# Rows of 1/rms through a store and a load in DRAM, in a two-layer decoder trunk

## The chip, the cores and the metric

The kernel runs on one core of a Trainium2 chip. The metric is the device time of one launch in microseconds (us). The engines are named as in the profile: PE (matrix products), PEld (loading of the stationary operand, beside PE), DVE (VectorE), ACT (ScalarE), POOL (GpSimd) and SP (SyncE, which only issues transfers here). Each engine takes its instructions in one order; transfers are issued by SP, POOL and once by ACT.

## The reference

The input x has 512 tokens of 1024 values. A layer, run twice, is three residual steps, and every step begins with the same norm:

```
r(x) = x * rsqrt(mean(x*x) + 1e-6) * g
x = x + 1/2 * (silu(r(x) @ Wg) * (r(x) @ Wu)) @ Wd        ffn1, inner width 2816
x = x + concat(A, B, C)(r(x) @ Win) @ Wout                mixer, three head groups
x = x + 1/2 * (silu(r(x) @ Wg') * (r(x) @ Wu')) @ Wd'     ffn2
```

After the second layer comes one more norm. What matters here is 1/rms = rsqrt(mean(x*x) + 1e-6), one number for each of the 512 tokens, needed six times: for ffn1, mixer and ffn2 of each layer. (The last norm is computed in another way and isn't touched.)

## The kernel before, in words

The activations stand with features on the partitions and tokens along the free dimension, so x is eight tiles of 128 x 512, held in four pairs. Every product is made of three matmuls of split operands (a high and a low part each). 1/rms of a token commutes with a product over the features, so the kernel multiplies by the gains first, starts the products at once, and puts 1/rms on the results. Two forms of it are kept:

- `rc`, the columns: 128 x 4, token 128n+p at partition p and column n. `norm_columns` (L221 to L231) makes it: eight small matmuls (L226) sum the squares `acc` over the partitions into a PSUM bank, DVE divides and adds epsilon (L228), and POOL raises to the power -0.5 (L230).
- `rr`, the rows: 128 x 512, the 512 values along the free dimension, the same on all partitions. `norm_rows` (L233 to L244) makes it from `rc`: for each of the four column groups DVE multiplies the identity by a column (L240, tile `dg`), PE multiplies a matrix of ones by that diagonal (L241, into the PSUM tile `psr`), and ACT copies the bank into `rr` (L243).

The feed-forward step (`ffn`, `gate_up`) works through 22 "quads" of weight blocks, gate and up in turn. For a quad SP and POOL fetch the weights (`fetch`, L111 to L116, `rawq`, two buffers; the POOL transfer of L112 adds into what SP has brought), ACT and DVE split them (`forms`, L89 and L90, into `wd`, `wa`, `wb`), PE makes seven products (L257 to L259, Strassen style, on the banks `pa`, `pb`, `pc`), and ACT and DVE gather them (`after`, L326 to L338) into a tile `g` or `u`, of which there are two each. When a quad is complete, `done` (L341 to L356) follows. For a gate quad DVE multiplies by `rr` (L347), ACT applies silu (L348) and DVE multiplies by `rr` again (L349). For an up quad DVE multiplies by the gate (L352) and the result is split into `h`. Products of `h` with the down weights (`pdn`) are threaded between the quads at written times (`schedule`).

Where the norm is made is set by the list `norms`: after each product one entry is taken from it and called. In the first feed-forward step of the kernel (`start`) the first two quads are computed from the input in another way, and `done` of both is itself an entry of that list; in the other three the list holds `norm_columns` at the third place and `norm_rows` at the sixth. In the mixer (`mixing`) the columns follow the first projection and the rows the second (L623 to L626); the first users of `rr` there are two multiplications of cosine and sine (L632, L633), which every query and key head needs, while `rc` scales the token-major projections. Instructions are put on their engines in an order that the tile framework chooses from the program's order and from what is ready.

Of the kernel before, what the change touches and what calls it, by code (L numbers as in the profile page):

```python
# [9 lines left out]
F32 = mybir.dt.float32  # L10
F32R = mybir.dt.float32r
AF = mybir.ActivationFunctionType
ALU = mybir.AluOpType
AX = mybir.AxisListType

P = 128
D = 1024
T = 512
# [4 lines left out]
NCH = T // P  # L23
# [25 lines left out]
def trunk(ctx, tc, xt, w_gu1, w_dn1, w_in, w_out, w_gu2, w_dn2, w_last, par, con, wst, bst, gain, out):  # L49
    nc = tc.nc  # L50
# [2 lines left out]
    wpool = ctx.enter_context(tc.tile_pool(name="wpool", bufs=1))  # L53
    spool = ctx.enter_context(tc.tile_pool(name="spool", bufs=2))
    pp = ctx.enter_context(tc.tile_pool(name="pp", bufs=8, space=bass.MemoryType.PSUM))
    stage = {}

    def bank(name):
        return pp.tile([P, T], F32, tag="ps", name=name)
# [6 lines left out]
    def uniq(s):  # L66
        uid[0] += 1
        return f"{s}{uid[0]}"
# [8 lines left out]
    ones = cpool.tile([P, P], F32, name="ones")  # L77
# [5 lines left out]
    ident = cpool.tile([P, P], F32, name="ident")  # L83
# [73 lines left out]
    state = {}  # L157
# [12 lines left out]
    def scratch(i, name):  # L170

        if stage["tags"] is None:
            return big(uniq(name))
        if i == 2:
            return stage["pool"].tile([P, 4 * T], F32, tag="hp", name=uniq(name), bufs=4)
        return stage["pool"].tile([P, 2 * T], F32, tag=stage["tags"][i], name=uniq(name), bufs=2)
# [55 lines left out]

    def norm_rows():  # L233

        rc = state["rc"]
        pr = bank(uniq("psr"))
        dg = scratch(2, "dg")
        for n in range(NCH):
            d = dg[:, n * P : (n + 1) * P]
            nc.vector.tensor_scalar(d, ident, rc[:, n : n + 1], None, ALU.mult)  # L240
            nc.tensor.matmul(pr[:, n * P : (n + 1) * P], lhsT=ones, rhs=d, start=True, stop=True)  # L241
        rr = spool.tile([P, T], F32, tag="rr", name=uniq("rr"), bufs=1)
        nc.scalar.copy(rr, pr)  # L243
        state["rr"] = rr  # L244


# [37 lines left out]
    def gate_up(w_gu, first, others, tail, from_start=False):  # L284
# [73 lines left out]
        if from_start:  # L358
            norms = start(w_gu, live, done)
            skip = lambda q, n: q < 2  # L360
        else:
            begin(0)
            begin(1)
            for m in range(KP):
                for q in (0, 1):
                    for n in (1, 2):
                        ps = psum(q, ("pa", "pb")[n - 1])
                        hi, lo = live[q]["w"][n]
                        bh, bl = form(m, MOVING[n])
                        c = slice(m * P, (m + 1) * P)  # L370
                        mm3(ps, hi[:, c], lo[:, c], bh, bl, m == 0, m == KP - 1, skip_group_check=True)
            for q in (0, 1):
                for n in (1, 2):
                    after(q, n)
            wait = lambda: None
            norms = [wait, wait, norm_columns, wait, wait, norm_rows]
            skip = lambda q, n: q < 2 and n < 3
        for _, kind, q, n in steps:
            if kind:
# [12 lines left out]
    def start(w_gu, live, done):  # L392
# [37 lines left out]
            squares(m)  # L430

        def rows():
            norm_rows()
            done(0)
            done(1)

        wait = lambda: None
        return [wait] * 5 + [norm_columns] + [wait] * 2 + [rows]

    def schedule(l, w_dn, hs):  # L440

# [134 lines left out]
    def mixing(l, after):  # L576
# [22 lines left out]
        def project(block, name):  # L599

            hi, lo = load(w_in[l, block])
            p = bank(uniq(name))
            for k in range(KT):
                c = slice(k * P, (k + 1) * P)
                mm3(p, hi[:, c], lo[:, c], xh(k), xl(k), k == 0, k == KT - 1)
            return p
# [15 lines left out]
        head = lambda w, h: qk[2 * w + h // 2][:, (h % 2) * T : (h % 2 + 1) * T]  # L622
        ahead = [project(0, "pqk")]  # L623
        norm_columns()
        ahead.append(project(1, "pqk"))
        norm_rows()  # L626
        rc, rr = state["rc"], state["rr"]
        for w in range(2):
            for h in range(HEADS):
# [16 lines left out]
        for n in range(NCH):  # L646
            p = bank(uniq("psc"))
# [248 lines left out]
```

## Time and profile before

| | us |
|---|---|
| median of 3 runs (1818.01 to 1818.21) | 1818.18 |
| the profiled execution, its own time | 1819.83 |
| span of the profiled execution | 1818.1 |
| mean granted TensorE clock, share of full | 0.998 |

The profile is of one execution. Times inside it count from the start of its span. A group of instructions has its line in the kernel, engine, operation and `out<-in` by the program's names; "x48" is a count. In the timeline the first number is the start and the second how long it took; what stands in brackets is the engine's idle time before it and what ended that. The chain is the work that ended last, followed back from the end of the kernel to what released each step.

### The profile page before, as it was taken

What the parts mean: (1) busy time and instruction counts of PE and PEld (TensorE: products, weight loads), DVE (VectorE), ACT (ScalarE), POOL (GpSimd) and SP (SyncE); (2) the same over time, 40 slices, a digit from 0 to 9 for tenths busy, and PEclk for the clock granted to TensorE, in tenths of its full rate; (3) what the DMA queues carried; (4) which work ended last, traced back from release to release, by engine and by line L of the source; (5) the groups of instructions that cost most, each with busy time, mean ns of one, the idle gap of its engine ahead of it and who ended that gap; (6) DMA issues with size and microseconds to landing.
All of it is one profiled execution on the core that took longest, in us unless ns stands there. A gap on an engine that the chain in (4) does not pass through costs nothing.

```text
span 1818.1 us, 28679 instructions
## 1 busy us (share of the span) xinstructions
PE 1804.7 (99%) x11704; PEld 1652.5 (91%) x11704; DVE 1329.5 (73%) x1818; ACT 830.8 (46%) x1222; POOL 121.0 (7%) x120
## 2 busy tenths in 40 slices
PE   9999999999999999999999999999999999999998
PEld 8999999888889999999899999998888899999997
DVE  7877777675667877777888777766658688777765
ACT  7544444423345544444655444444143555444444
POOL 0100000000100000000000000000000000000000
PEclk9999999999999999999999999999999999999999
DMA  7665555522222855555447555563222157565632
GB/s 215 175 174 150 147 149 152 177 88 82 70 93 76 214 152 151 157 157 156 128 130 192 147 148 151 151 189 116 100 75 80 58 134 199 155 157 157 157 88 81
DMA packets 120339, 251.20 MB, mean 138 GB/s; under 512 B 9744, under 2 KB 11792, under 8 KB 119696
## 3 DMA queue, kind: packets, MB, share of 16 engines
q1 hardware_dynamic: 96672, 204.25, 35.0%
q0 software_dynamic: 23392, 45.09, 15.0%
q8 instruction: 91, 1.49, 0.3%
q14 instruction: 40, 0.33, 0.1%
q10 hardware_dynamic: 144, 0.04, 0.0%
HBM read 247.24 MB, written 2.10 MB: 137 GB/s over the span
## 4 chain that ended last, share of the span: by engine, by line
PE 96%; DVE 2%; ACT 1%; issue 0%; DMA 0%; POOL 0%; POOLq 0%; SPq 0%; ACTq 0%
PE pa L257 9%; PE pa L259 9%; PE pa L258 9%; PE pdn L150 8%; PE pdn L151 8%; PE pdn L152 8%; PE pc L258 4%; PE pc L259 4%; PE pc L257 4%; PE pb L257 2%; PE pb L259 2%; PE pb L258 2%; PE pqk L150 2%; PE pqk L152 2%; PE pout L151 2%; PE pout L150 2%
## 5 line engine op out<-in xcount | busy, mean ns | idle before, releaser
L150 PE MATMUL pdn<-h,wdn 128*128 128x512 f32 x632 | 247.6, 392 | 0.0
L151 PE MATMUL pdn<-h,wdn 128*128 128x512 f32 x632 | 247.6, 392 | 0.0
L152 PE MATMUL pdn<-h,wdn 128*128 128x512 f32 x632 | 246.0, 389 | 0.3 <-DVE wdn L90 0.3
L89 ACT CAST wd<-rawq 128x1024 fp32r<-128x1024 f32 (+1 forms) x172 | 135.2, 832 | 172.0 <-PE pc L259 167.4
L257 PE MATMUL pa<-xf,wa 128*128 128x256 f32 x688 | 195.5, 284 | 0.8 <-ACT g L326 0.8
L258 PE MATMUL pa<-xf,wa 128*128 128x256 f32 x688 | 194.9, 283 | 0.0
L259 PE MATMUL pa<-xf,wa 128*128 128x256 f32 x688 | 194.9, 283 | 0.0
L90 DVE TENSOR_TENSOR wd<-rawq,wd 128x1024 fp32r<-128x1024 f32 (+1 forms) x172 | 157.5, 955 | 49.1 <-ACT wd L89 48.7
L112 POOL DMA_DIRECT2D rawq<-in_w_gu x86 | 94.3, 1096 | 1260.6 <-DMA rawq<-in_w_gu 436.6
L89 ACT CAST wdn<-rawd 128x512 fp32r<-128x512 f32 (+1 forms) x152 | 97.2, 640 | 176.8 <-PE pdn L152 174.1
L89 ACT CAST w<-raw 128x1024 fp32r<-128x1024 f32 x77 | 80.9, 1051 | 196.1 <-PE pqk L152 60.6
L152 PEld LDWEIGHTS pdn<-h,wdn 128*128 128x128 f32 x632 | 118.7, 188 | 26.5 <-DVE wdn L90 0.7
L90 DVE TENSOR_TENSOR w<-raw,w 128x1024 fp32r<-128x1024 f32 x77 | 94.1, 1223 | 64.4 <-ACT w L89 63.7
L150 PEld LDWEIGHTS pdn<-h,wdn 128*128 128x128 f32 x632 | 119.2, 189 | 21.1
L151 PEld LDWEIGHTS pdn<-h,wdn 128*128 128x128 f32 x632 | 119.2, 189 | 19.5
L257 PEld LDWEIGHTS pa<-xf,wa 128*128 128x128 f32 x688 | 132.4, 192 | 1.8 <-ACT g L326 1.2
L90 DVE TENSOR_TENSOR wdn<-rawd,wdn 128x512 fp32r<-128x512 f32 (+1 forms) x152 | 107.2, 705 | 35.3 <-ACT wdn L89 35.2
L259 PEld LDWEIGHTS pa<-xf,wa 128*128 128x128 f32 x688 | 132.3, 192 | 0.0
L258 PEld LDWEIGHTS pa<-xf,wa 128*128 128x128 f32 x688 | 132.3, 192 | 0.0
L282 DVE SCALAR_TENSOR_TENSOR x<-pdn,x 128x512 f32<-128x512 f32 x152 | 104.0, 685 | 3.8 <-PE pdn L152 3.8
L90 DVE TENSOR_TENSOR wa<-rawq,wa 128x1024 fp32r<-128x1024 f32 x86 | 104.9, 1219 | 1.8 <-ACT wa L89 1.8
L90 DVE TENSOR_TENSOR wb<-rawq,wb 128x1024 fp32r<-128x1024 f32 x86 | 104.8, 1219 | 1.2 <-ACT wb L89 1.2
(289 smaller groups left out, 5080.5 us busy)
## 6 DMA issues: line engine op xcount, KB each, us to landing
rawq<-in_w_gu SPq DMA_DIRECT2D x172, 512.0 KB, 5.4
rawq<-in_w_gu POOLq DMA_DIRECT2D x86, 512.0 KB, 5.7
rawd<-in_w_dn SPq DMA_DIRECT2D x140, 256.0 KB, 4.4
raw<-in_w_in SPq DMA_DIRECT2D x52, 512.0 KB, 3.5
rawq<-in_w_gu SPq DMA_DIRECT2D x86, 256.0 KB, 5.8
raw<-in_w_out SPq DMA_DIRECT2D x16, 512.0 KB, 3.5
rawd<-in_w_dn SPq DMA_DIRECT2D x12, 384.0 KB, 3.3
raw<-in_w_last SPq DMA_DIRECT2D x6, 512.0 KB, 4.0
```

Of the source, the lines that this page charges most:

```text
L89: nc.scalar.copy(hi, src)
L90: nc.vector.tensor_tensor(lo, src, hi.bitcast(F32), ALU.subtract)
L112: nc.gpsimd.dma_start(two[:, :, 1, :], src.rearrange("p (n s c) -> p n s c", n=2, s=2)[:, :, 0, :], accum_op=ALU.add)
L150: nc.tensor.matmul(ps, lhsT=ah, rhs=bh, start=first, stop=False, **kw)
L151: nc.tensor.matmul(ps, lhsT=ah, rhs=bl, start=False, stop=False, **kw)
L152: nc.tensor.matmul(ps, lhsT=al, rhs=bh, start=False, stop=last, **kw)
L257: nc.tensor.matmul(ps, lhsT=hi[:, c], rhs=bh, start=one, stop=False, skip_group_check=True)
L258: nc.tensor.matmul(ps, lhsT=hi[:, c], rhs=bl, start=False, stop=False, skip_group_check=True)
L259: nc.tensor.matmul(ps, lhsT=lo[:, c], rhs=bh, start=False, stop=m == pairs[-1], skip_group_check=True)
L282: nc.vector.scalar_tensor_tensor(x[d], p, 0.5, x[d], ALU.mult, ALU.add)
```

## The change

`norm_rows` no longer uses DVE, PE and ACT. POOL issues a store of the 128 x 4 columns to a tile in DRAM, laid out so that the 512 values follow each other, and SP issues a load of these 2 KB onto each of the 128 partitions. The rows are now made right after the columns in all six places: in the three later feed-forward steps this moves `norm_rows` three entries earlier; in the first one the columns go one entry later and `done` of the first two quads two entries later; in the mixer the rows are made before the second projection, and a third projection is put ahead of the first use of `rr`.

```diff
+    dpool = ctx.enter_context(tc.tile_pool(name="dpool", bufs=2, space=bass.MemoryType.DRAM))
...
     def norm_rows():
-        rc = state["rc"]
-        pr = bank(uniq("psr"))
-        dg = scratch(2, "dg")
-        for n in range(NCH):
-            d = dg[:, n * P : (n + 1) * P]
-            nc.vector.tensor_scalar(d, ident, rc[:, n : n + 1], None, ALU.mult)
-            nc.tensor.matmul(pr[:, n * P : (n + 1) * P], lhsT=ones, rhs=d, start=True, stop=True)
+        row = dpool.tile([NCH, P], F32, tag="row", name=uniq("row"))
+        nc.gpsimd.dma_start(row.rearrange("n p -> p n"), state["rc"])
         rr = spool.tile([P, T], F32, tag="rr", name=uniq("rr"), bufs=1)
-        nc.scalar.copy(rr, pr)
+        nc.sync.dma_start(rr, row.rearrange("n p -> (n p)").unsqueeze(0).broadcast_to([P, T]))
         state["rr"] = rr
...
-            norms = [wait, wait, norm_columns, wait, wait, norm_rows]
+            norms = [wait, wait, lambda: (norm_columns(), norm_rows())]
...
         def rows():
-            norm_rows()
             done(0)
             done(1)
...
-        return [wait] * 5 + [norm_columns] + [wait] * 2 + [rows]
+        return [wait] * 6 + [lambda: (norm_columns(), norm_rows())] + [wait] * 3 + [rows]
...
         ahead = [project(0, "pqk")]
         norm_columns()
+        norm_rows()
         ahead.append(project(1, "pqk"))
-        norm_rows()
+        ahead.append(project(2, "pqk"))
         rc, rr = state["rc"], state["rr"]
```

## Rows read from the trace of the kernel before

**Rows 1.** The page, part 1: busy time and share of each engine.
```profile
PE 1804.7 (99%) x11704; PEld 1652.5 (91%) x11704; DVE 1329.5 (73%) x1818; ACT 830.8 (46%) x1222; POOL 121.0 (7%) x120
```
**Rows 2.** The page, part 4: shares of the chain that ended last.
```profile
PE 96%; DVE 2%; ACT 1%; issue 0%; DMA 0%; POOL 0%; POOLq 0%; SPq 0%; ACTq 0%
```
**Rows 3.** Waits of PE: us in total, times, longest.
```profile
PE pss L226 <- DVE acc L219: 0.9, 1, 0.9
PE pa L257 <- ACT g L326: 0.8, 1, 0.8
```
**Rows 4.** Tiles psr and dg: count, ns least/median/most, first and last start.
```profile
L241 PE MATMUL psr<-dg,ones x48: 270/275/275, 52.1 to 1479.2; 128*128 128x128 f32 x48
L240 DVE TENSOR_SCALAR dg<-ident,rc x24: 277/282/289, 50.1 to 1473.4; 128x128 f32<-128x128 f32 x24
```
**Rows 5.** The chain in order of time, pieces of psr: start, us.
```profile
373.61 0.89 PE psr L241 x8
...
581.90 0.22 PE psr L241 x2
...
583.40 0.67 PE psr L241 x6
```
**Rows 6.** Timeline of a later feed-forward norm (ffn2 of the first layer).
```profile
575.63 1.03 POOL L230 TENSOR_TENSOR rc<-ms,mhalf 128x4 f32<-128x4 f32 x1 [3.52 <-DVE ms L228]
...
581.92 0.37 SPq L111 DMA_DIRECT2D rawq<-in_w_gu  x1
...
585.95 1.23 DVE L347 TENSOR_TENSOR g<-g,rr 128x1024 f32<-128x1024 f32 x1 [0.87 <-ACT g L338]
...
587.42 1.22 DVE L90 TENSOR_TENSOR wa<-rawq,wa 128x1024 fp32r<-128x1024 f32 x1
...
591.11 0.28 PE L257 MATMUL pa<-xf,wa 128*128 128x256 f32 x1
```
**Rows 7.** Timeline of the first mixer's norm.
```profile
368.27 1.04 POOL L230 TENSOR_TENSOR rc<-ms,mhalf 128x4 f32<-128x4 f32 x1 [5.14 <-DVE ms L228]
...
375.91 0.69 DVE L632 TENSOR_TENSOR side<-ct,rr 128x512 f32<-128x512 f32 x1
```
**Rows 8.** The page, parts 3 and 6: a queue; issues, KB each, us to landing.
```profile
q0 software_dynamic: 23392, 45.09, 15.0%
...
rawq<-in_w_gu POOLq DMA_DIRECT2D x86, 512.0 KB, 5.7
...
raw<-in_w_in SPq DMA_DIRECT2D x52, 512.0 KB, 3.5
```
**Rows 9.** DMA issues of the whole span, further down the list.
```profile
out<-o SPq DMA_DIRECT2D x8, 256.0 KB, 2.2
```
**Rows 10.** DMA issues in the stretch 46 to 58 us alone.
```profile
rawd<-in_w_dn SPq DMA_DIRECT2D x2, 256.0 KB, 6.7
```
**Rows 11.** Timeline of the first norm of the kernel (POOL, DVE and ACT).
```profile
48.09 1.96 POOL L230 TENSOR_TENSOR rc<-ms,mhalf 128x4 f32<-128x4 f32 x1 [8.26 <-DVE ms L228]
51.48 1.14 POOL L112 DMA_DIRECT2D rawq<-in_w_gu  x1 [1.43 <-DMA rawq<-in_w_gu]
...
53.81 2.36 DVE L347 TENSOR_TENSOR g<-g,rr 128x1024 f32<-128x1024 f32 x2 [0.34 <-ACT rr L243]
...
56.31 1.06 ACT L348 ACTIVATE g<-g 128x1024 f32<-128x1024 f32 x1
...
57.40 1.23 DVE L349 TENSOR_TENSOR g<-g,rr 128x1024 f32<-128x1024 f32 x1 [0.84 <-ACT g L348]
...
59.68 1.22 DVE L352 TENSOR_TENSOR u<-u,g 128x1024 f32<-128x1024 f32 x1
...
61.88 0.36 ACT L326 COPY g<-pa 128x256 f32<-128x256 f32 x1
```
**Rows 12.** Windows: stretch, us; PE, PEld, DVE, ACT, POOL busy; clock, DMA share, GB/s.
```profile
48.00:51.00 3.00, 3.00 (x17) 3.00 (x16) 2.02 (x5) 0.00 (x0) 1.96 (x1) 0.50 0.78 236
51.00:51.40 0.40, 0.40 (x4) 0.40 (x4) 0.40 (x4) 0.00 (x0) 0.00 (x0) 0.52 1.06 353
```

## The prediction

> **What bounds the kernel now.** I read the shares by engine first, then the chain, then what PE waits for. PE shows as busy for 99% of the span [rows 1], and the chain that ended last runs through PE for 96% of it [rows 2]: this is a PE-bound kernel, and a PE instruction taken out is worth its own step, as long as nothing that PE needs becomes late. Since a busy PE can hide stalls inside its pipeline, the list of its waits is the better witness: at the two places that concern us, both behind the first norm, there are only 0.9 us before the sums of squares and 0.8 us before a product that needs a bank read out by ACT [rows 3]. In the five later norms PE stops for nothing that touches the norm. So there are two regimes: five norms in a stretch where PE alone counts, and the first norm, which stands on the chain with POOL, DVE and ACT.
>
> **What is removed.** The 48 matmuls of `psr` are eight per norm at 275 ns, but matmuls overlap, so their duration isn't their price [rows 4]. The chain shows the step: 0.89 us for eight in a mixer, 0.22 + 0.67 = 0.89 us in a feed-forward norm [rows 5]. Five later norms give 5 x 0.89 = **4.45 us**. The 24 DVE multiplications of 0.28 us [rows 4] and the six ACT copies lie beside PE and give nothing by themselves; DVE stood idle while it waited for the columns anyway.
>
> **What is added: the row's way through DRAM.** No store of four-byte pieces is in this trace, so I bound it. A POOL transfer of 512 KB lands 5.7 us after its issue [rows 8]. That queue's 23392 packets took 15.0% of 16 engines' 1818 us, which is 4363 us or 0.187 us per packet [rows 8]; 86 transfers make 272 packets each, 17 per engine, 3.2 us; so 2.5 us are left that don't depend on the size. The new store has 512 pieces, 32 per engine and one at the end. If a four-byte packet took as long as a 2 KB one, the store would land after 2.5 + 33 x 0.187 = 8.7 us. From below, the kernel's output store lands in 2.2 us [rows 9]. I take 2.5 us and 0.05 us per packet, **4.2 us**, nearer to the lower end because four bytes are little to move. The load of 2 KB onto 128 partitions is 256 KB: a 512 KB weight load lands in 3.5 us in quiet, a 256 KB one in 6.7 us in the crowded stretch behind the first norm, and 2.2 us is the fastest transfer of all [rows 8 to 10]. I take **3.5 us**. The row is then there 7.7 us after the columns, with 4.4 and 15.4 us as the ends.
>
> **The three later feed-forward norms.** Take the one at 575 us [rows 6]. The columns end at 575.63 + 1.03 = 576.66 us, and the first user of the row starts at 585.95 us, which becomes 585.06 us when PE is 0.89 us quicker: 8.4 us after the columns. The row at 7.7 us is in time, by 0.7 us. If it is later, DVE waits, and what is late next is the split of `wa` that stands behind on DVE: it ends at 588.64 us and PE uses it at 591.11 us, so another 2.5 us are free. PE is touched only when the row takes over 10.9 us. SP now waits for the store before it issues the load, and behind that wait stands the next weight fetch at 581.92 us; the store has landed by 576.66 + 4.2 = 580.9 us, so the fetch isn't held (at the upper end it is, by 3.4 us). Moving the rows three entries earlier costs nothing: the queue slots it passes on PE and DVE are its own. Cost taken: nothing.
>
> **The two mixers.** The first user of the row starts 6.6 us after the columns [rows 7], so a row after 7.7 us is 1.1 us late for DVE. The third projection, put ahead of it, gives PE work that needs no row, and the projections have banks to stand in. I cost it at nothing; with the cover gone it is at most that lateness.
>
> **The first norm.** Here the row matters at once. POOL ends the columns at 50.05 us; today DVE uses the row at 53.81 us, and from there runs the way on which PE waits: first multiplication (half of 2.36 = 1.18 us), silu 1.06, second multiplication 1.23, gate times up 1.22, then the ACT copy of 0.36 us that can only write its tile when the gate has been used; it ends at 61.88 + 0.36 = 62.24 us [rows 11], and PE's 0.8 us of waiting ends there [rows 3]. The bare links sum to 5.05 us; today they are spread over 8.4 us because other work of DVE and ACT stands between. After the change that other work can be done while the row is on its way, so I take the bare links. The load shares the stretch with weight transfers: I put it at 4.4 us, a quarter of the way from 3.5 to 6.7, since by the time the store has landed, at 54.3 us, most of these are through. The row is there at 50.05 + 4.2 + 4.4 = 58.65 us, and PE is released at 63.7 us instead of 62.24: **1.5 us later**. POOL's weight transfer at 51.48 us [rows 11] goes behind the store and is about as late as that takes to issue, some 1.1 us by its own row; the splits it feeds come after the hole anyway. Now PE's own gains in this stretch: the eight matmuls, and the 0.9 us before the sums, which the later place of the columns may remove. They only make PE reach the hole sooner, so I count them as nothing; if the row came early they would count.
>
> The clock belongs here too. After PE's stop at the sums, the granted clock fell to 0.50 for 48 to 51 us, and 0.52 until 51.4 [rows 12], the lower of its two levels, 1.2 GHz. Half speed for 3.4 us costs 1.7 us. The hole in front of the released product will be some microseconds long, longer than the stop that preceded this drop, so I expect one such stretch behind it: **1.7 us**, with 0 and 3.4 as the ends.
>
> **The sum.** 4.45 saved, 1.5 + 1.7 lost: 1.25 us less. The profiled execution took 1819.83 us for a span of 1818.1; the sum on it gives 1818.6. That execution stands 1.65 us above the median of the runs, 1818.18, so the forecast for the median is **1816.9 us**, 0.07% less: no change, within the 0.2% (3.6 us) that a measurement of this kernel can tell.
>
> **The rivals.**
>
> *The start is covered (faster).* If the row needs about 6.3 us, it is there at 56.3 us, PE is released at 61.35 us, 0.9 us earlier than today, and there is no hole to lower the clock: 4.45 + 0.9 = 5.3 us less, 1812.9. For it speaks that the fastest transfers land in 2.2 us, against it the crowd in the first norm's stretch. The Trainium skill, page "DMA: Bandwidth & Descriptors", section "Anatomy of one DMA", fits 2.0 us plus bytes over 436e3 per transfer: by it the store takes 2.0 and the load 2.6 us (estimates), the row is there at 54.7 us, and the time would be about 1811. The POOL row, with 2.5 us besides its packets, agrees with that constant roughly; the 6.7 us of the weight load do not.
>
> *The store is slow (slower).* One mechanism: 512 pieces of four bytes land late, and four feed-forward norms wait for the row. Let it need X us after the columns. The first norm loses 50.05 + X + 5.05 - 62.24 + 1.7 = X - 5.4, the three others X - 10.9 each above that, and 4.45 come back. The total passes 3.6 us slower at X = 11.5. At X = 14 it is 8.6 + 9.3 - 4.45 = 13.4 us slower, 1831.6. For it speaks the upper end of the store, against it that the end takes four bytes for as dear as 2 KB. The same page of the Trainium skill, section "Rules for kernel authors", speaks against this change: a strided last dimension lowers to one descriptor per element, and one should rearrange it. No run here shows what such an element costs.
>
> *The freed time isn't returned.* If DVE or the weight loads set the pace right behind the five norms, nothing comes back there and the start's 3.2 us remain: 1821.4. Against it: PE's list of waits has no entry there [rows 3].
>
> **How the numbers follow.** The forecast has 0.38 (rows between 7 and 11 us, a range of its own of 1814.5 to 1818.5), the covered start 0.37, the slow store 0.20, the time not returned 0.05. Faster by over 0.2% is the covered start, 0.37; within 0.2% the forecast and the time not returned, 0.43; slower 0.20. The range that leaves out 2 in 10 goes down to 1812.0, past the covered start's own value, and up to 1823.5, where the row needs about 12 us: most of the slow store lies above.
>
> **What would show it.** PE without `psr`, and five norms in which PE's waits stay empty; the user of the row in the norm near 575 us waiting for ACT, as now, and not for a transfer; the store landing near 4.2 us and the load near 3.5; behind the first norm a hole in PE of several microseconds that a transfer ends through DVE and ACT, and a stretch at half clock after it. I am wrong if that hole is not there, if the store takes 7 us or more, or if PE waits in the later norms.

## The result and the profile after

The changed kernel takes 1871.08 us (median of four runs, 1869.29 to 1872.78) beside 1818.2 us for the kernel before on the same chip (1818.01 to 1818.29): a ratio of 1.0284, with 1.0271 to 1.0296 as the 95% interval. It is 52.9 us slower; forecast were 1816.9 us, with 1823.5 as the upper end of the range. The profiled span is 1870.8 us instead of 1818.1. Beside the experiments below the kernel before was run again; its runs lie near 1818 or near 1820 us, with medians of 1818.4 to 1819.9, and the ratios there are to these.

The first two lines are from the page of the kernel after: busy time and share of each engine, and the shares of the chain that ended last.

```profile
PE 1816.3 (97%) x11656; PEld 1659.5 (89%) x11656; DVE 1321.8 (71%) x1794; ACT 827.7 (44%) x1216; POOL 126.7 (7%) x126
...
PE 87%; DMA 6%; DVE 4%; ACT 1%; issue 1%; POOL 1%; SPq 0%; POOLq 0%; DVEq 0%; ACTq 0%
```

PE has 48 instructions fewer than in [rows 1], as meant, yet is busy 11.6 us longer (part of its work runs at half clock, as shown below), and transfers, which held 0% of the chain in [rows 2], now hold 6% of it. Next, the waits of PE in the kernel after (us in total, times, longest), which answer to [rows 3]:

```profile
PE pqk L153 <- DVE w L91: 17.2, 2, 8.8
PE pa L253 <- ACT g L322: 11.5, 3, 4.4
PE pa L253 <- DVE u L330: 9.9, 1, 9.9
...
PE pa L253 <- ACT u L322: 2.5, 3, 1.6
```

The two long waits for `w` are the two mixers, the 9.9 us for `u` are the first norm, and those for ACT's copies of `pa` follow the three later feed-forward norms. All six norms stop PE, where before there were only the two stops of 0.9 and 0.8 us at the first. The issues of the two new transfers (KB each, median us from issue to landing) show why the row is late:

```profile
rr<-row SPq DMA_DIRECT2D x6, 256.0 KB, 4.8
row<-rc POOLq DMA_DIRECT2D x6, 2.0 KB, 8.6
```

The store of 2 KB takes almost twice as long as the load of 256 KB. Three timelines show what became of it. The first norm of the kernel after, to be held against [rows 11]:

```profile
48.49 1.96 POOL L231 TENSOR_TENSOR rc<-ms,mhalf 128x4 f32<-128x4 f32 x1 [8.21 <-DVE ms L229]
50.76 0.83 POOL L237 DMA_DIRECT2D row<-rc  x1 [0.30 <-POOL rc L231]
...
61.41 0.34 SPq L239 DMA_DIRECT2D rr<-row  x1
...
65.01 2.36 DVE L343 TENSOR_TENSOR g<-g,rr 128x1024 f32<-128x1024 f32 x2 [10.49 <-DMA rr<-row]
...
67.29 0.41 DVE L330 TENSOR_TENSOR u<-u,pa 128x256 f32<-128x256 f32 x1
...
67.76 0.58 PE L253 MATMUL pa<-xf,wb 128*128 128x256 f32 x1 [9.85 <-DVE u L330]
```

The norm of the second feed-forward block of layer 0, to be held against [rows 6]:

```profile
597.62 1.03 POOL L231 TENSOR_TENSOR rc<-ms,mhalf 128x4 f32<-128x4 f32 x1 [3.62 <-DVE ms L229]
599.01 0.83 POOL L237 DMA_DIRECT2D row<-rc  x1 [0.36 <-POOL rc L231]
...
607.70 0.34 SPq L239 DMA_DIRECT2D rr<-row  x1
608.14 0.38 SPq L112 DMA_DIRECT2D rawq<-in_w_gu  x1
...
614.17 1.23 DVE L343 TENSOR_TENSOR g<-g,rr 128x1024 f32<-128x1024 f32 x1 [7.09 <-DMA rr<-row]
...
616.80 0.58 PE L253 MATMUL pa<-xf,wa 128*128 128x256 f32 x1 [4.32 <-ACT g L322]
```

And the first mixer, to be held against [rows 7]:

```profile
379.24 1.04 POOL L231 TENSOR_TENSOR rc<-ms,mhalf 128x4 f32<-128x4 f32 x1 [5.99 <-DVE ms L229]
380.65 0.83 POOL L237 DMA_DIRECT2D row<-rc  x1 [0.37 <-POOL rc L231]
...
390.36 0.33 SPq L239 DMA_DIRECT2D rr<-row  x1
...
394.60 0.69 DVE L628 TENSOR_TENSOR side<-ct,rr 128x512 f32<-128x512 f32 x1 [14.09 <-DMA rr<-row]
...
403.38 1.23 DVE L91 TENSOR_TENSOR w<-raw,w 128x1024 fp32r<-128x1024 f32 x1
...
404.66 0.79 PE L153 MATMUL pqk<-xf,w 128*128 128x512 f32 x1 [8.76 <-DVE w L91]
```

The row is used 14.6, 15.5 and 14.3 us after the columns end (65.01 - 50.45, 614.17 - 598.65, 394.60 - 380.28), where 7.7 us were forecast. In the mixer, look at what stands between 394.60 and 403.38 us: 13 DVE instructions, all of them users of the row or of what is made from it, and only then the split of the next projection's weights, for which PE has been waiting.

The clock adds its part. Windows of the kernel after around that stop (columns as in [rows 12], so the granted clock is the third number from the end):

```profile
394.00:399.00 5.00, 1.90 (x9) 1.24 (x7) 4.34 (x7) 1.05 (x1) 0.00 (x0) 1.00 0.02 7
399.00:404.00 5.00, 0.00 (x0) 0.00 (x0) 4.88 (x8) 0.00 (x0) 0.00 (x0) 0.66 0.00 0
404.00:409.00 5.00, 4.34 (x10) 3.47 (x11) 4.94 (x8) 0.00 (x0) 0.00 (x0) 0.50 0.34 105
409.00:414.00 5.00, 5.00 (x19) 3.98 (x18) 2.32 (x4) 1.06 (x1) 0.00 (x0) 0.81 0.64 212
```

While PE stands still the granted clock falls, and it is at 0.50, the level of 1.2 GHz, when PE starts again at 404.66 us; it is back only within the last window. By an estimate from these windows 4.34 x 0.50 + 5 x 0.19 = 3.1 us go this way, on top of the stop of 8.8 us; less the 0.9 us of the matmuls that is the mixer's loss, 11.0.

To see where the 52.7 us of span lie, I took the start of the `rc` instruction on POOL at each norm, and the distances between them. This measure is used for every run below.

| stretch | before | after | difference |
|---|---|---|---|
| start to first norm | 48.09 | 48.49 | +0.40 |
| first norm to first mixer | 320.18 | 330.75 | +10.57 |
| first mixer to the norm of ffn2, layer 0 | 207.36 | 218.38 | +11.02 |
| to the norm of ffn1, layer 1 | 345.15 | 352.10 | +6.95 |
| to the second mixer | 342.99 | 348.44 | +5.45 |
| second mixer to the norm of ffn2, layer 1 | 207.29 | 217.84 | +10.55 |
| to the end | 347.04 | 354.80 | +7.76 |

So the first norm has cost 10.6 us, the two mixers 21.6, and the three later feed-forward norms 20.2, each net of PE's saved steps.

### The profile page after: what moved, and what is told of

It reads as the page before. It is cut to its first block, busy times and chain, and to the rows that moved or that the text cites. A ratio compares the mean times of both kernels' runs of the same rounds, so it can differ in the third digit from the quotient of the medians.

```text
span 1870.8 us, 28569 instructions
## 1 busy us (share of the span) xinstructions
PE 1816.3 (97%) x11656; PEld 1659.5 (89%) x11656; DVE 1321.8 (71%) x1794; ACT 827.7 (44%) x1216; POOL 126.7 (7%) x126
## 3 DMA queue, kind: packets, MB, share of 16 engines
q1 hardware_dynamic: 97536, 205.82, 34.5%
q0 software_dynamic: 23584, 45.11, 15.1%
## 4 chain that ended last, share of the span: by engine, by line
PE 87%; DMA 6%; DVE 4%; ACT 1%; issue 1%; POOL 1%; SPq 0%; POOLq 0%; DVEq 0%; ACTq 0%
PE pdn L151 8%; PE pdn L152 8%; PE pdn L153 8%; PE pa L253 8%; PE pa L255 8%; PE pa L254 8%; PE pc L255 4%; PE pc L253 4%; PE pc L254 4%; DMA row<-rc 3%; DMA rawq<-in_w_gu 2%; PE pb L255 2%; PE pb L254 2%; PE pb L253 2%; PE pout L151 2%; PE pout L153 2%
## 5 line engine op out<-in xcount | busy, mean ns | idle before, releaser
L253 PE MATMUL pa<-xf,wa 128*128 128x256 f32 x688 | 198.1, 288 | 14.1 <-ACT g L322 11.5
L254 PE MATMUL pa<-xf,wa 128*128 128x256 f32 x688 | 196.8, 286 | 0.0
L255 PE MATMUL pa<-xf,wa 128*128 128x256 f32 x688 | 196.8, 286 | 0.0
L253 PEld LDWEIGHTS pa<-xf,wa 128*128 128x128 f32 x688 | 134.1, 195 | 16.4 <-ACT g L322 12.4
L255 PEld LDWEIGHTS pa<-xf,wa 128*128 128x128 f32 x688 | 134.2, 195 | 0.0
L254 PEld LDWEIGHTS pa<-xf,wa 128*128 128x128 f32 x688 | 134.2, 195 | 0.0
L343 DVE TENSOR_TENSOR g<-g,rr 128x1024 f32<-128x1024 f32 x44 | 53.8, 1225 | 90.9 <-ACT g L334 60.6
L253 PE MATMUL pa<-xf,wb 128*128 128x256 f32 x344 | 98.2, 286 | 9.9 <-DVE u L330 9.9
L91 DVE TENSOR_TENSOR wa<-rawq,wa 128x1024 fp32r<-128x1024 f32 x86 | 104.9, 1219 | 3.1 <-ACT wa L90 3.1
```

Of the source, the lines that this page charges most:

```text
L91: nc.vector.tensor_tensor(lo, src, hi.bitcast(F32), ALU.subtract)
L253: nc.tensor.matmul(ps, lhsT=hi[:, c], rhs=bh, start=one, stop=False, skip_group_check=True)
L254: nc.tensor.matmul(ps, lhsT=hi[:, c], rhs=bl, start=False, stop=False, skip_group_check=True)
L255: nc.tensor.matmul(ps, lhsT=lo[:, c], rhs=bh, start=False, stop=m == pairs[-1], skip_group_check=True)
L343: nc.vector.tensor_tensor(c3, c3, rr, ALU.mult)
```

## The experiments

Each group asks one thing. The kernels have the numbers that the expectations use (there is no fifth). Distances are those of the table, in its order from the first norm on, unless a run's own are given.

### Is the wait for the row the whole loss?

In the third kernel nothing is stored; the row is loaded from an input, in the same form. This load waits for nothing, so it goes well ahead of the columns (the first one at 12.9 us) and the row is never late.

```diff
-        nc.gpsimd.dma_start(row.rearrange("n p -> p n"), state["rc"])
...
-        nc.sync.dma_start(rr, row.rearrange("n p -> (n p)").unsqueeze(0).broadcast_to([P, T]))
+        nc.sync.dma_start(rr, gain[0:1, :T].broadcast_to([P, T]))
```

> No store; the load of 2 KB onto 128 partitions reads a row of an input and so waits for nothing (1/rms in the rows is left out; the columns stay). All of the change but the store and the wait for it is there. Theory A (all of the loss is the wait for the row, and PE's freed steps are returned): 4.5 us saved in the five later norms and up to 3 us at the first one, 1810 to 1814 us. Rival D (the freed PE time is not returned, something else sets the pace): 1817 to 1819 us. Rival E (the change of order, the earlier rows and the third projection ahead, costs by itself): over 1820 us.

Measured: 1813.09 us (1812.70 to 1814.35), ratio 0.9967 (0.9955 to 0.9980). The five stretches behind the later norms are 206.43, 344.36, 342.21, 206.35 and 346.63 us, that is 0.93, 0.79, 0.78, 0.94 and 0.41 less than before. PE's saved steps are given back, 3.85 us of the 4.45, and the new order by itself costs nothing; everything that is lost hangs on the store and on the wait for it. What the load costs at the norm itself this kernel doesn't show, since its loads go earlier; the fourteenth does.

### What makes the store slow?

The first kernel stores the same 2 KB in pieces of 16 bytes, one per partition; the row's tokens then stand in another order.

```diff
-        nc.gpsimd.dma_start(row.rearrange("n p -> p n"), state["rc"])
+        nc.gpsimd.dma_start(row.rearrange("n p -> (n p)").rearrange("(p n) -> p n", n=NCH), state["rc"])
```

> This kernel stores the 128 x 4 columns as they lie, 16 contiguous bytes per partition, so the 512 values of the row come in another order (the token order is left out; the times are not touched by it). Theory A (the four-byte pieces make the store late: 32 of them per engine): with 8 pieces of 16 bytes per engine the store lands about 4.0 us after its issue (2.5 us plus 8 times 0.19) instead of 8.6, the row is some 4.6 us earlier in all six norms, and the kernel takes 1840 to 1850 us. Rival B (a write to DRAM from the POOL queue takes 8.6 us whatever its pieces): landing 8 to 9 us, kernel 1869 to 1873 us.

Measured: 1828.2 us, quicker than theory A said (1840 to 1850), as the store lands in 2.2 us and not in 4.0. The issues of the two transfers and PE's longest waits in it:

```profile
rr<-row SPq DMA_DIRECT2D x6, 256.0 KB, 4.4
row<-rc POOLq DMA_DIRECT2D x6, 2.0 KB, 2.2
```
```profile
PE pa L253 <- DVE u L330: 5.4, 1, 5.4
PE pqk L153 <- DVE w L91: 4.8, 2, 2.5
```

With a quarter of the pieces the store lands in 2.2 us instead of 8.6, 43 us of the 53 are gone, and the stretches behind the three later feed-forward norms (344.37, 342.22, 346.91) are below those of before. What is left stands at the first norm and in the mixers.

The second kernel leaves the pieces and changes the queue: the store is issued from SP.

```diff
-        nc.gpsimd.dma_start(row.rearrange("n p -> p n"), state["rc"])
+        nc.sync.dma_start(row.rearrange("n p -> p n"), state["rc"])
```

> The same store of 512 four-byte pieces, issued by SP instead of POOL. Theory A (the pieces): it still lands 7 to 9 us after its issue, and the kernel takes 1866 to 1873 us. Rival C (the POOL queue is what is slow): it lands in 2.2 to 4 us, as the output store of SP does, and the kernel takes 1840 to 1850 us.

Measured: 1885.36 us, outside what was expected; the store lands after 9.5 us. So it isn't POOL's queue that makes it slow. That it became worse was not foreseen; PE now has one wait of 15.0 us for a split of `wb`. On SP the store's own wait for the columns stands ahead of the fetches as well, which would explain it, but no run here shows that by itself.

In the eighth kernel PE transposes the columns, ACT copies them into a tile of four partitions, and the store writes four pieces of 512 bytes.

```diff
+        nc.tensor.transpose(pt[:NCH, :P], state["rc"], ident)
...
+        nc.scalar.copy(four, pt[:NCH, :P])
+        nc.gpsimd.dma_start(row, four)
```

> The change with the columns turned on PE first (one transpose of 128 x 4 into 4 x 128, a small copy by ACT), so that the store moves four contiguous rows of 512 bytes and the row is in its right order. Theory A (the pieces): the store lands in 2 to 3 us, the row is later than in the run with the flat store only by transpose and copy, about 1 us, and the kernel takes 1828 to 1836 us. Rival B2 (what was quick in the flat store is that each partition writes one piece, and four partitions alone are slow): the store lands in 5 us or more, and the kernel takes 1845 us or more.

Measured: 1831.52 us, as expected. The store lands in 1.8 us, the load in 3.1. The price moved to PE, which now waits for the columns in order, at all six norms:

```profile
PE prt L238 <- POOL rc L231: 8.3, 6, 2.5
```

The Trainium skill, page "DMA: Bandwidth & Descriptors", section "Rules for kernel authors", warns that a strided last dimension becomes one descriptor per element. The packets of the second kernel agree: SP's queue has 100704 in it and 97536 in the changed kernel, that is 528 more for each of the six stores. The runs give the price that the page doesn't: 8.6 us in 512 pieces, 2.2 in 128, 1.8 in four. By the fit of the same page's section "Anatomy of one DMA" (2.0 us plus bytes over 436e3), which the page gives for transfers issued from GpSimd, 2 KB take 2.0 us, an estimate that holds for the last two forms and is wrong by a factor of four for the first. It does not cover the load, which SP issues: there the prediction's 2.6 us go beyond the page, and 4.8 were measured.

What exactly makes the first form slow stays open. A store from POOL adds 32 packets to its queue in all three forms (23584 packets instead of 23392 for six stores), so packets are not the measure; and the number of pieces, their size and how far they lie apart in DRAM change together in these kernels.

### The mixers

The fourth kernel gives the mixers their rows by matmuls, in the old place, and leaves the other four norms changed.

```diff
-        norm_rows()
...
-        ahead.append(project(2, "pqk"))
+        norm_rows_pe()
```

> The two mixers make their rows as the kernel before does (diagonals, matmuls, copy, at the old place); the four feed-forward norms are as changed. Theory A2 (in the mixers the wait holds DVE, the split of the fourth projection's weights stands behind it, and PE stops: 11 us per mixer as the distances between the norms in the two profiles show): about 1849 us (1846 to 1852). Rival F (the mixers lose nothing of their own, what the profile shows there comes from elsewhere): 1868 to 1873 us.

Measured: 1851.66 us, and 207.35 and 207.29 us in the mixers, as before. The two together account for 19.4 us of the 52.9.

The sixth kernel tries whether lateness can be covered by order alone, with the slow store: in the feed-forward blocks the users of the row are put behind the third quad's last subtraction on DVE, in the mixers six projections are issued ahead and the row's users put behind the sixth split.

```diff
+                if q == 2 and not from_start:
+                    with tc.issue_after(state["c22"].ins):
+                        done(0)
+                        done(1)
...
+                if q > 1:
+                    done(q)
...
+        for b in range(2, 6):
+            ahead.append(project(b, "pqk"))
...
+                    with tc.issue_after(state["split"].ins):
```

> The slow store of four-byte pieces stays, from POOL; only the users of the row move behind on DVE. In the three later feed-forward steps the finishing of the first two quads is queued on DVE behind a gathering step of the third quad; in the mixers six projections stand ahead of the first users, and these are queued behind the sixth split of weights. The first norm stays as changed. Theory A3 (not the lateness of the row costs, but what is queued behind its users on DVE): the five later stretches get as short as in the run without a store, the first norm keeps its loss of 13.6 us against that run, 1824 to 1830 us. Rival G (a late row costs wherever its users stand, for example because SP holds its weight loads while it waits for the store): 1850 us or more.

Measured: 1864.04 us, far above what theory A3 said and within rival G's range. The mixers come to 211.4 and 212.9 us, a little over half of their loss back (11.9 of 21.6 us); the feed-forward stretches stay at 353.98, 350.65 and 354.91. So in the feed-forward blocks it was not the readers' place on DVE alone.

### The first norm

The seventh kernel is the sixth with the first norm's rows by matmuls.

```diff
+            norm_rows_pe()
...
-        return [wait] * 6 + [lambda: (norm_columns(), norm_rows())] + [wait] * 3 + [rows]
+        return [wait] * 5 + [norm_columns] + [wait] * 2 + [rows]
```

> As the run before this one, and the first norm makes its rows as the kernel before does, with diagonals and matmuls at the old place. Theory A3: the first norm as before, five later norms with PE's 0.89 us returned: 1813.5 to 1816 us. Rival G: 1835 us or more. If it is between 1817 and 1819, the steps of PE are not returned when a store is in the way.

Measured: 1846.32 us, ratio 1.0149 (1.0134 to 1.0164). The stretch behind the first norm is 320.21 us again. But behind the later feed-forward norms 351.6, 348.2 and 353.4 us stay, and its trace gave me a new theory, from SP's timeline:

```profile
590.92 0.34 SPq L252 DMA_DIRECT2D rr<-row  x1
591.35 0.38 SPq L112 DMA_DIRECT2D rawq<-in_w_gu  x1
```

The columns of that norm ended at 581.16 us. SP, which works in order, stood at the store until 590.92 us, and the next fetch of weights went 10.2 us after the columns; in [rows 6] it goes 5.3 us after them. I took that wait for the cause.

### What the later feed-forward norms lose

The tenth kernel is the seventh with the load put behind that fetch in SP's order (in the mixers behind that of the fifth projection's weights).

```diff
+        with tc.issue_after(state["loaded"].ins):
+            nc.sync.dma_start(rr, row.rearrange("n p -> (n p)").unsqueeze(0).broadcast_to([P, T]))
...
-            norms = [wait, wait, lambda: (norm_columns(), norm_rows())]
+            norms = [wait, wait, lambda: (norm_columns(), norm_rows())] + [wait] * 5 + [load_rows]
```

> As the seventh kernel (first norm in the old way, users of the row later on VectorE), with one thing moved: in the three later FFN norms the load of the row is put into SyncE's order behind the next fetch of a quad's weights (line 112 and its fellows), so that SyncE's wait for the store no longer holds that fetch. Theory H (what the FFN norms lost in the seventh kernel is SyncE standing at the store while the weights wait): the fetch goes about 6.3 us behind the columns as before, no wait of TensorE of over 1 us is left there, the distances that follow the three norms come back from 351.6, 348.2 and 353.4 to 344.4 to 345.5, 342.2 to 343.3 and 346.6 to 347.6 us, and the time falls from 1846.3 to 1825 to 1830 us (the mixers still lose their 8.8). Rival G (lateness of the row itself, through the gate buffers that come free later, costs the FFN its time): the distances stay over 350, 347 and 352, the time over 1841 us.

Measured: 1842.88 us; 349.76, 346.75 and 349.62 us. The fetch goes in time (588.90 us, 5.3 after the columns), and the loss stays for the most part. Theory H falls as the whole cause. Yet 7.1 us come back in these three stretches, so with the whole row loaded the order of load and fetch is worth that much; the mixers, at 214.03 and 212.26, lose 2.9 of it again. The time itself lies in rival G's range. The eleventh kernel adds an even order in the mixers:

```diff
+        for b in (5, 6, 7):
+            ahead.append(project(b, "pqk"))
+            with tc.issue_after(state["split"].ins):
...
+                heads(2)
+        heads(2)
```

> As the tenth kernel, and in the mixers five projections instead of six are issued ahead of the first rotation and then two heads' rotations follow each further projection's split, so that no split stands behind more than two heads. Theory: the mixers' loss is splits of weights queued on VectorE behind the row's users and nothing else, so both mixers come to 206.4 to 207.4 us (before: 207.3; with the row from elsewhere: 206.4) and the whole to 1815.0 to 1818.5 us, at or just below the kernel before. Rival: the late row costs the mixers in any order (the rotations must be caught up while TensorE needs splits at the same rate): they stay at 209 to 212 us and the time at 1821 to 1828 us.

Measured: 1828.99 us (1826.82 to 1831.05), ratio 1.0049 (1.0035 to 1.0062). The mixers are at 206.43 and 206.36 us, to 0.01 us what they were with no store at all. The load stands in SP's order where the tenth kernel has it, and there the mixers got nothing back: so their loss was the order on DVE, even with a store of 9 us. The total missed its forecast by the feed-forward norms alone (350.88, 346.67, 350.11), and its timelines say where to look:

```profile
581.38 0.37 SPq L112 DMA_DIRECT2D rawq<-in_w_gu  x1
...
588.18 0.34 SPq L257 DMA_DIRECT2D rr<-row  x1
```
```profile
576.47 0.82 POOL L250 DMA_DIRECT2D row<-rc  x1 [0.36 <-POOL rc L231]
589.33 1.12 POOL L113 DMA_DIRECT2D rawq<-in_w_gu  x1 [12.04 <-DVE g L342]
```

POOL's transfer adds onto what the fetch of 581.38 us brings, and goes 8.0 us behind it, at 589.33 us; in the kernel before it goes 5.6 us behind (581.92 to 587.50). The fetch's own landing took 7.3 us instead of 4.8, to just after that of the store, at 588.18 us, where SP's load is released. Two kernels that change nothing but add transfers to the kernel before tell the rest. The first stores the columns and loads half of the row into a tile that nobody reads:

```diff
+        row = dpool.tile([NCH, P], F32, tag="row", name=uniq("row"))
+        nc.gpsimd.dma_start(row.rearrange("n p -> p n"), state["rc"])
+        r2 = spool.tile([P, H], F32, tag="r2", name=uniq("r2"), bufs=1)
+        nc.sync.dma_start(r2, row.rearrange("n p -> (n p)")[:H].unsqueeze(0).broadcast_to([P, H]))
```

> The kernel before, with its rows by matmuls as they were, and beside them at all six norms the store of the columns from GpSimd and a load from it on SyncE into a tile of 256 columns that nobody reads. Nobody waits for the row, only SyncE waits for the store. Theory H (SyncE's wait by itself delays the next weights): the first fetch behind each FFN norm goes at the store's landing, 10 to 11 us behind the columns instead of 6.3, the distances that follow the three FFN norms grow by 2 to 7 us each, the whole to 1826 to 1842 us. Rival (only VectorE's order matters; a row that nobody reads costs nothing): 1817.5 to 1820 us, distances within 0.5 us of before.

Measured: 1842.28 us; first norm and mixers as before (320.54, 207.35, 207.36), the feed-forward norms at 354.04, 350.71 and 353.09 us. What they lose is lost with no reader. The second is the same without the two lines of the load:

> The kernel before, its rows by matmuls, and beside them at all six norms the four-byte store alone: no load, so nobody waits for anything. Theory H (the FFN norms lose because SyncE stands at the store) and theory L (because the row's load comes in among the fetches of weights): nothing happens, 1817.5 to 1820 us, distances within 0.5 us of before, fetches behind an FFN norm landing in 5.5 to 6 us. Theory S (the store itself, for the 8 to 11 us until it lands, holds up the transfers issued beside it): the first fetch behind it lands in about 8 us, the one that adds on GpSimd's queue starts 2 to 3 us late, the distances that follow the FFN norms grow by 2 us or more each, the whole to 1824 to 1836 us.

Measured: 1838.25 us, above even theory S's range (up to 1836), and 352.38, 349.09 and 353.05 us behind the feed-forward norms: +7.2, +6.1 and +6.0, though nobody waits for this store. First norm and mixers lose nothing (319.33, 207.35, 207.36). The issues in the 15 us around the norm of ffn2, layer 0, first in the kernel before (574.6 to 589.6 us):

```profile
rawq<-in_w_gu SPq DMA_DIRECT2D x2, 512.0 KB, 5.3
...
rawq<-in_w_gu SPq DMA_DIRECT2D x1, 256.0 KB, 5.9
```

and then with the store beside it (573.4 to 588.4 us), with the SP, POOL and ACT instructions of that stretch:

```profile
rawq<-in_w_gu SPq DMA_DIRECT2D x2, 512.0 KB, 11.9
rawq<-in_w_gu SPq DMA_DIRECT2D x1, 256.0 KB, 12.5
row<-rc POOLq DMA_DIRECT2D x1, 2.0 KB, 9.4
```
```profile
580.72 0.37 SPq L112 DMA_DIRECT2D rawq<-in_w_gu  x1
```
```profile
575.81 0.83 POOL L238 DMA_DIRECT2D row<-rc  x1 [0.36 <-POOL rc L231]
592.80 1.10 POOL L113 DMA_DIRECT2D rawq<-in_w_gu  x1 [16.17 <-DMA rawq<-in_w_gu]
```
```profile
593.60 1.57 ACT L90 CAST wd<-rawq 128x1024 fp32r<-128x1024 f32 x2 [4.14 <-DMA rawq<-in_w_gu]
```

The fetch is issued in time, 5.3 us after the columns, and lands 11.9 us later instead of 5.3: 7.4 us after the store has landed (575.81 + 9.4 = 585.2, 580.72 + 11.9 = 592.6). So behind the four-byte store other transfers crawl, and not only until it has landed. One window of each kernel shows it, first before, then with the store (the last number is GB/s):

```profile
586.00:588.00 2.00, 2.00 (x19) 2.00 (x19) 2.00 (x3) 1.88 (x2) 0.50 (x1) 1.00 0.77 283
```
```profile
586.00:588.00 2.00, 2.00 (x19) 2.00 (x19) 2.00 (x3) 1.98 (x2) 0.00 (x0) 1.00 0.60 49
```

ACT and DVE wait for the weights, then PE does. In the mixers the same store makes a fetch land after 10.4 us instead of 3.5, and costs nothing there, since those weights are not needed so soon.

The last of the series keeps SP's wait and shrinks the load to one partition.

```diff
-        nc.sync.dma_start(r2, row.rearrange("n p -> (n p)")[:H].unsqueeze(0).broadcast_to([P, H]))
+        nc.sync.dma_start(r2[0:1, :], row.rearrange("n p -> (n p)")[:H].unsqueeze(0))
```

> The kernel of the unread row, with the load cut from 128 partitions to one (1 KB instead of 128 KB): SyncE still waits for the store, but no transfer of size comes in. Theory H: as with the load on all partitions, 1836 to 1843 us, the distances that follow the FFN norms at 350 or more, 347 or more, 349 or more. Theory L (the size of the load among the fetches): within 2 us of before. Theory S (the store alone): what the kernel with the store alone shows, within 2 us.

Measured: 1839.14 us; 351.76, 348.83 and 353.50 us. That is within 1 us of the store alone, as theory S has it. Theory H's ranges would fit it as well; what tells them apart is the thirteenth kernel, which loses the same with no wait on SP at all. The wait adds nothing to the store because the weights are late either way: POOL's transfer, which adds onto the fetch, goes 17.3 us after the columns here (594.24 - 576.99), 17.4 with the store alone (592.80 - 575.45), and 10.8 in the kernel before (587.50 - 576.66). The size of the unread load, half of a row, is worth 3 us (1842.28 against 1839.14). How the one transfer holds up the others the trace doesn't show. The records of the store's own packets end within some 2 us, long before it lands; what happens in the rest of its 9 us, and after them, stays open.

### Is the saving to be had otherwise?

The ninth kernel is the kernel before with the four matmuls of a chunk each made one of 512 columns.

```diff
-            nc.tensor.matmul(pr[:, n * P : (n + 1) * P], lhsT=ones, rhs=d, start=True, stop=True)
+        nc.tensor.matmul(pr, lhsT=ones, rhs=dg[:, :T], start=True, stop=True)
```

> The kernel before, with one matmul of ones with all four diagonals side by side (512 columns) in place of four with 128 columns; no DRAM. If a step of PE goes by its columns at the rate of the products of 512 columns (0.23 us for one, and two per call as now), the eight steps of 0.89 us become two of 0.46: six times 0.43 us less, 1815 to 1816 us. Rival: the step of a matmul of this type goes by columns in such a way that 512 columns cost as much as four times 128, and nothing changes: 1817.5 to 1818.7 us.

Measured: 1819.72 us, ratio 1.0003 (0.9994 to 1.0013): no change. Tile psr in it (ns least, median, most):

```profile
L241 PE MATMUL psr<-dg,ones x12: 590/592/667, 50.8 to 1475.9; 128*128 128x512 f32 x12
```

Two instructions of 592 ns stand where eight of 275 stood. In the chain they take 0.86 us (at 580.52 us) where the eight took 0.89 [rows 5]: here the price goes by the columns, not by the count.

The fourteenth kernel uses what was found. The store keeps a partition's four values together, the row arrives in the order partition, chunk, and every user on DVE reads it with a stride of four elements; the first norm keeps its matmuls; the mixers have the even order of the eleventh kernel.

```diff
-        nc.gpsimd.dma_start(row.rearrange("n p -> p n"), state["rc"])
+        nc.gpsimd.dma_start(row.rearrange("n p -> (n p)").rearrange("(p n) -> p n", n=NCH), state["rc"])
...
-        state["rr"] = rr
+        state["rr"] = rr.rearrange("q (p n) -> q n p", n=NCH)
...
-                rr = state["rr"].unsqueeze(1).broadcast_to([P, 2, T])
+                rr = state["rr"].unsqueeze(1).broadcast_to([P, 2, NCH, P])
```

> A version put together from what was found: the store keeps each partition's four values together (16 bytes, landing in about 2.2 us as in the first experiment), the row arrives in the order partition, chunk, and every user on VectorE reads it with a stride of four elements; first norm by the matmuls as before; FFN users where the change has them; mixers with two heads' rotations behind each further split. Theory: first norm 320.2 as before, mixers 206.4, distances that follow the FFN norms 344.4 to 345.2, 342.2 to 343.0, 346.7 to 347.4, the whole 1814.5 to 1817 us, just under the kernel before (ratio 0.997 to 0.9995). Rival: the strided reads slow VectorE's 1.23-us products by half or more, and the time lands at 1818 us or above.

Measured: 1814.62 us (1814.31 to 1816.34), ratio 0.9974 (0.9964 to 0.9985), with 320.20, 206.43, 344.37, 342.23, 206.36 and 346.73 us. It beats both kernels. Its issues at the norm of ffn2, layer 0 (573.8 to 588.8 us):

```profile
rawq<-in_w_gu SPq DMA_DIRECT2D x2, 512.0 KB, 5.3
...
rr<-row SPq DMA_DIRECT2D x1, 256.0 KB, 3.4
...
row<-rc POOLq DMA_DIRECT2D x1, 2.0 KB, 2.6
```

The fetch beside this store lands in 5.3 us, as with no store, and the load at the norm itself costs PE nothing. The strided readers do cost DVE something, as the groups of instructions say (busy time, mean ns; the groups in the kernel before had 1225 and 1219 ns):

```profile
L363 DVE TENSOR_TENSOR g<-g,rr 128x1024 f32<-128x1024 f32 x44 | 81.5, 1852 | 0.8 <-ACT g L362 0.8
...
L361 DVE TENSOR_TENSOR g<-g,rr 128x1024 f32<-128x1024 f32 x44 | 81.1, 1844 | 62.3 <-ACT g L352 61.5 <-ACT rr L244 0.5
```

Half as much again, some 55 us of DVE in all, and none of it reaches PE.

## Why the prediction was wrong, step by step

**The bound and what is removed: right.** PE bounds this kernel, and taking its eight matmuls out of five norms was put at 4.45 us. The kernel without a store gives 3.85 and the fourteenth 3.71, most norms 0.8 to 0.9; the last of them gives 0.3 to 0.4.

**The store: the term that was mis-sized.** It was taken at 4.2 us, "nearer to the lower end because four bytes are little to move"; it measured 8.6 in the median, near the upper end of 8.7, and 10.6 at the first norm. There was no row for four-byte pieces in the trace, and between the two ends I chose by what a piece carries. That the upper end comes so close is luck: it reckoned 33 packets per engine, the trace has two (32 for a store on 16 engines), and by the same sum the pieces of 16 bytes would land after 4.0 us and not after 2.2. The load was 4.8 us instead of 3.5, and 3.6 in the first norm instead of 4.4. Together the row came 14 to 15.5 us after the columns, not 7.7: the slow-store rival, which I gave 0.20 with X = 14.

**That rival was priced too low.** At X = 14 it said 1831.6; the time was 1871. Four things were missing in it.

*The two mixers, "I cost it at nothing; with the cover gone it is at most that lateness".* This step failed most. The row was 7.7 us late there (14.3 us instead of 6.6), and each mixer lost 11. I had counted PE's work that needs no row, and not what DVE has queued behind the row's users: the whole backlog of rotations and then the split that PE needs. The sixth kernel gave a little over half back by order, the eleventh all of it.

*The three feed-forward norms, "PE is touched only when the row takes over 10.9 us".* By this the row's 15.5 us cost 4.6, and the stop in the trace is 4.3 us long and ends behind the row's reader: the path may be right, but it is not the whole account. With no reader of the row at all the stretch is lost all the same, since the store keeps the next weights from landing; what a late row costs here without such a store no run shows. Here the prediction had no term for what the new transfer does to those that were there; I had only asked whether SP would hold the fetch, and said that it does so at the upper end by 3.4 us. It did, by 4.2 (608.14 - 598.65 = 9.5 us after the columns, where [rows 6] have 5.3). By the kernels with the unread row that wait alone costs nothing beside the store; with the whole row loaded ahead of the fetch the order was worth 7.1 us (seventh to tenth kernel).

*The clock, counted once.* It was priced for the first norm, at 1.7 us. The profile after shows half clock behind all six norms: the granted clock is 0.50 at 68 to 76 us, 404 to 410, 618 to 622, 968 to 970, 1322 to 1328 and 1536 to 1540.

*The first norm.* By X - 5.4, with the 14.6 us of this norm, it was to lose 9.2 us with the clock; it lost 10.6. That X was off is not all, and that the rest comes so close is luck, since two terms were off in opposite ways. PE's stop was not ended by the ACT copy behind silu, gate and second product, 5.05 us after the row, but by a subtraction on DVE that reads the bank `pa` and stands behind the row's first users (67.29 us in the timeline above): 2.75 us after the row (67.76 - 65.01). And half clock lasted until 76 us, so that some 7.5 us of PE's work ran at it; by an estimate from that 3.7 us went to the clock, where 1.7 were priced.

**The rivals.** The covered start fell with the store; "the freed time isn't returned" fell in the third kernel. What I had named as a sign of error, a store of 7 us or more and waits of PE in the later norms, is what the profile shows.

**The sum of the causes**, each by its own run: the mixers 19.4 us (fourth kernel), the feed-forward norms 17.3 (store alone: 7.2 + 6.1 + 6.0, less the 2.0 that PE saves in these stretches by the kernel without a store), the first norm 10.0 (sixth to seventh kernel, 330.18 to 320.21). Together 46.7 us of the 52.7; the other 6.0 were not pursued.

## What to carry to other kernels

Where a transfer is added to a schedule in which other transfers feed the bound engine, price it three times: its own landing, what it does to the transfers beside it, and what is queued in order behind whoever waits for it. A small store is not always a cheap one: try it in whole pieces (here 16 bytes per partition instead of four times four) and let the reader take the stride. And a store that nobody waits for, added to the old kernel, is the cleanest way to see the second price.

## What the runs showed of the hardware that was not expected

- 2 KB in 512 pieces of four bytes land after 8.6 us from POOL (8.3 to 10.6 in the changed kernel) and 9.5 from SP; in 128 pieces of 16 bytes after 2.2; in four of 512 bytes after 1.8.
- Behind such a store 512 KB fetches that land in 5.3 and 3.5 us otherwise take 11.9 and 10.4; the first of these was issued 4.9 us after the store and landed 7.4 us after it had landed.
- A DVE product of 128 x 1024 whose second operand is read with a stride of four elements takes 1.84 us instead of 1.23.
- Two fp32 matmul instructions of 512 columns cost as much as eight of 128: 0.86 us of the chain against 0.89.
